# Layer 0 in emission order: attention pairs advance hop by hop between later products, another order of the weight stream, and the last addition moved

## The chip, the core and the metric

The kernel runs on one core of a Trainium2 chip. Its engines run side by side, each with its own queue of instructions in a fixed order, joined by semaphores: TensorE (PE: matmul and transposition; PEld: loading of its weights), VectorE (DVE), ScalarE (ACT), GpSimd (POOL) and SyncE (SP), which issues most transfers. The metric is the device time of one execution in microseconds (us). The profile is taken from one execution.

## What is computed

A decoder trunk of two layers over 256 tokens, width 1024, all in float32, cut here to what matters:

```python
def even_layer(x, mem_n, ...):                       # layer 0
    h = rms_norm(x, norm_g)
    (nq, nkc, nvc, nks, nvs, nkw, nvw, ng, nz, mq, mk, mv, mz, eq, ez) = _split(h @ w_in, EVEN_SPLITS)
    kc = nsa_compress(rot(nkc), pe_k, w1_k, w2_k)
    vc = nsa_compress(heads(nvc), pe_v, w1_v, w2_v)
    gates = jax.nn.sigmoid(ng + gate_b)...
    a_out = nsa_attention(rot(nq), kc, vc, rot(nks), heads(nvs), rot(nkw), heads(nvw), gates)
    b_out = moba_attention(rot(mq), rot(mk), heads(mv))
    m_out = memory_attention(heads(eq), mem_n, w_mem_kv)
    y = jnp.concatenate([a_out * silu(nz), b_out * silu(mz), m_out * silu(ez)], axis=-1) @ w_out
    return x + y

def odd_layer(x, mem_n, ...):                        # layer 1
    h = rms_norm(x, norm_g)
    rq, rk, rv, rz, eq, ez = _split(h @ w_in, ODD_SPLITS)
    ...                                              # retention, 4 heads, and the memory attention again
    return x + y

def reference(...):
    mem_n = rms_norm(mem, mem_norm_g)
    x = even_layer(x, mem_n, ...)
    x = odd_layer(x, mem_n, ...)
    return rms_norm(x, final_norm_g)
```

With 256 tokens the selected blocks and the window of the sparse attention cover all earlier tokens, and the block attention has one block, its own. So each reduces to causal attention: two branches (selected, window) for four pairs of sparse heads, one for four pairs of block heads. The compressed branch has 15 blocks. The memory attention has four heads (two pairs) over 256 memory tokens.

## The kernel before

**Products.** A product multiplies the activations by a 1024x512 piece of weights, which come in four transfers ("units") of 128x1024. Each operand is a sum of a high and a low part in TensorE's fast float type (fp32r), and each product is three matmuls, high times high, high times low, low times high (`mm3`, L138 to L142). The activations are split once. Each unit of weights is split on the chip by `split`: a cast on ScalarE (`whi`, L127) and a subtraction on VectorE (`wlo`, L128). `project` gives tokens on the partitions (two banks of 512 columns, one for each half of the tokens), `project_turned` gives features on the partitions.

**Layer 0.** The first product (`nz`, the sparse group's gate) is written out by hand with the first transfers; its two `pj` banks are read by `gate_path` (L332), once the row scales are known (`rsqrt`, L112; spread over the partitions by L192, copied by L194). Then come `sparse_keys`, `sparse_queries`, `compress` (280 columns: keys and values to compress and the gates; eight additions at L555 put them in the form that two rows of small matmuls take, side by side in the two halves of the array), `memory_queries`, `compressed_scores`, `block_gates`, `block_keys`, `memory_rows`, sparse pairs 0 to 2, the memory keys and attention, `block_queries`, `block_values`, sparse pair 3, four block pairs, and the output product.

**An attention pair** (`causal_pair`, L428; `mem_attention`, L467) handles two heads. TensorE computes the scores of two halves of the tokens (L402, L403); VectorE adds the mask and takes the maxima (L435); ScalarE takes exponentials with their sums (L437); VectorE and ScalarE scale by the inverse sum and the gate (L441 to L448); TensorE transposes (`transposes`, L199); ScalarE copies to `pt` (L449, L492); TensorE multiplies with the values, the two heads side by side in two column halves (`side_by_side`, L105, tile 128x64); `gated` multiplies by the gate and splits the result. A score has the high part of the query in 64 of the 128 rows and its low part in the other 64 (`stack_q`, L341), against the keys stacked likewise (`stack_k`, L348): ScalarE, VectorE and GpSimd prepare these, and each score is two fp32r matmuls.

**What sets the order.** Outside the first transfers a scheduler orders the instructions on every engine from the program's dependencies. Buffers are rings by name: 12 of `v4` (128x1024), three of `whi` and `wlo`, six raw ones, and eight PSUM banks:

```python
BANKS = {"pj": 3, "tr": 1, "s": 2, "t": 1, "o": 1}
```

**The end.** The last product is finished bank by bank (L741 to L747): the two halves of token half 0, the first half of token half 1, and the second half of it in a part of 256 columns and a last one of 256, in a bank of its own. For each, VectorE adds the residual (L879; L876 for the last), ScalarE sums squares (L881); then the root, its inverse (L889), the scaling (L890, L891) and the transfers out (L892, L893).

Of the kernel before, what the change touches and what calls it, by code (L numbers as in the profile page):

```python
# [16 lines left out]
P = 128  # L17
# [4 lines left out]
NV = 12  # L22
NRAW = 6
CUT = 256
BANKS = {"pj": 3, "tr": 1, "s": 2, "t": 1, "o": 1}
# [28 lines left out]
def trunk(  # L54
# [68 lines left out]
    def split(raw, cols, tag=None):  # L123

        hi = tl(tag or "whi", [P, 1024], NV if tag else 3, F32R)[:, :cols]
        lo = tl(tag or "wlo", [P, 1024], NV if tag else 3, F32R)[:, :cols]
        S.copy(hi, raw)  # L127
        V.tensor_tensor(lo, raw, hi.bitcast(F32), ALU.subtract)  # L128
        return hi, lo

    def units(src, idx, cols):

        for u in range(4):
            raw = ahead.pop(0) if ahead else load(tl("raw", [P, 1024], NRAW)[:, : 2 * cols], src[idx + u // 2][:, (u % 2) * 2 * cols : (u % 2 + 1) * 2 * cols])
            wh, wl = split(raw, 2 * cols)
            yield 2 * u, wh, wl

    def mm3(ps, lh, ll, rh, rl, start, stop, shared=False):  # L138

        PE.matmul(ps, lh, rh, start=start, stop=False, skip_group_check=shared)  # L140
        PE.matmul(ps, lh, rl, start=False, stop=False, skip_group_check=shared)  # L141
        PE.matmul(ps, ll, rh, start=False, stop=stop, skip_group_check=shared)  # L142

    def project(src, idx, lhs, cols=512, tag="pj"):

        hi, lo = lhs
        ps = [bank(tag) for _ in range(2)]
        for k0, wh, wl in units(src, idx, cols):
            for tok in range(2):
                for j in range(2):  # L150
# [3 lines left out]
                    mm3(ps[tok][:, :cols], hi[:, kt, ts], lo[:, kt, ts], wh[:, cs], wl[:, cs], kt == 0, kt == KT - 1)  # L154
        return [p[:, :cols] for p in ps]
# [10 lines left out]
    def project_turned(src, idx, lhs):  # L166

        ps = [bank("pj") for _ in range(2)]
        for kt, wh, wl in units(src, idx, 512):
            turned_unit(ps, lhs, wh, wl, (kt, kt + 1), range(4))  # L170
        return ps

    def project_mem(src, idx, lhs):
# [3 lines left out]
        for k0, wh, wl in units(src, idx, 512):  # L177
            turned_unit(ps, lhs, wh, wl, (k0, k0 + 1), range(2))
            for tok in range(2):
# [6 lines left out]
        return ps  # L186

# [28 lines left out]
    def gain_split(raw, g, hi, lo, k0, kts):  # L216
        for kt in kts:
            r = raw[:, kt - k0]
            S.activation(hi[:, kt], r, AF.Copy, scale=g[:, kt : kt + 1])  # L219
            V.scalar_tensor_tensor(lo[:, kt], r, g[:, kt : kt + 1], hi[:, kt].bitcast(F32),  # L220
                                   op0=ALU.mult, op1=ALU.subtract)
# [20 lines left out]
    for tag, shape, bufs, dt in (  # L242
        ("whi", [P, 1024], 3, F32R), ("wlo", [P, 1024], 3, F32R), ("y", [P, 2, 4, T], 2, F32R), ("pt", [P, 2, 512], 2, F32),
        ("ym", [P, 2, 2, T], 1, F32R), ("s2", [P, 2, T], 6, F32), ("rot_a", [P, 512], 2, F32), ("rot_b", [P, 512], 1, F32),
# [24 lines left out]
    for q in range(4):  # L269
        gain_split(xraw[q // 2], vect[:, V_G0 : V_G0 + 8], xh, xl, 4 * (q // 2), range(2 * q, 2 * q + 2))  # L270
# [8 lines left out]
    def row_scale(rows, rstd, width):  # L279
        ss = tl("ss", [P, 2], 2)  # L280
        for tok in range(2):
            S.activation(rows[tok], rows[tok], AF.Square, accum_out=ss[:, tok : tok + 1])
        V.tensor_scalar(ss, ss, 1.0 / width, EPS, op0=ALU.mult, op1=ALU.add)
        rsqrt(rstd, ss, 2)

# [4 lines left out]


    row_scale(xrow, rstd0, D)
# [36 lines left out]
    def gate_path(ps, rb, szT):  # L329

        z = tl("tmp2", [P, 512], 3).rearrange("p (k t) -> p k t", k=2)
        V.scalar_tensor_tensor(z, ps.rearrange("p (k t) -> p k t", k=2), 0.5,  # L332
                               rb.unsqueeze(1).to_broadcast([P, 2, T]), op0=ALU.mult, op1=ALU.mult)
        S.activation(szT, z, AF.Tanh)
        V.scalar_tensor_tensor(szT, szT, 1.0, z, op0=ALU.add, op1=ALU.mult)
# [5 lines left out]
    def stack_q(dst, src):  # L341

        for i in range(2):
            own, other = slice(64 * i, 64 * i + 64), slice(64 - 64 * i, 128 - 64 * i)
            S.copy(dst[own, :, i], src[own])
            V.tensor_tensor(dst[other, :, i], src[own], dst[own, :, i].bitcast(F32), ALU.subtract)

    def stack_k(dst, lo, src):  # L348

        for i in range(2):  # L350
            own, other = slice(64 * i, 64 * i + 64), slice(64 - 64 * i, 128 - 64 * i)
            S.copy(dst[own, :, i], src[own])
            V.tensor_copy(dst[other, :, i], dst[own, :, i].bitcast(F32))
            V.tensor_tensor(lo[own, :, i], src[own], dst[own, :, i].bitcast(F32), ALU.subtract)  # L354
            G.tensor_copy(lo[other, :, i], lo[own, :, i].bitcast(F32))  # L355

    def mem_query(ps, rb, dst):
        e = tl("tmp2", [P, 512], 3).rearrange("p (k t) -> p k t", k=2)
        scaled(ps, rb, 0.125, e)
        stack_q(dst, e)  # L360

    szn = tl("v4", [P, 4, T], NV)
    for i in range(2):
        gate_path(ps_n[i], rb0, szn[:, 2 * i : 2 * i + 2])


    def rot_transpose(ps, name, done):

        for tok in range(2):
            r = rotate(ps[tok], tabs[name][0][:, tok], tabs[name][1][:, tok], 8, 32)  # L370
            b = transposes([r[:, i * P : (i + 1) * P] for i in range(4)], "tr")
            done(b.rearrange("p (k t) -> p k t", t=P), slice(tok * P, (tok + 1) * P))

    def heads_q(ps, plain=None):

        dst = [tl("v4", [P, 2, 2, T], NV, F32R) for _ in range(2)]

        def done(b, ts):
            for i in range(2):
                stack_q(dst[i][:, :, :, ts], b[:, 2 * i : 2 * i + 2])  # L380
            if plain is not None:
                S.copy(plain[:, :, ts], b)

        rot_transpose(ps, "q", done)
        return dst

    def heads_k(ps):
        dst = [tl("v4", [P, 2, 2, T], NV, F32R) for _ in range(2)]
        lo = [tl("v4", [P, 2, 2, T], NV, F32R) for _ in range(2)]

        def done(b, ts):
            for i in range(2):
                stack_k(dst[i][:, :, :, ts], lo[i][:, :, :, ts], b[:, 2 * i : 2 * i + 2])

        rot_transpose(ps, "k", done)
        return dst, lo

    SPAN = (slice(0, P), slice(P, 3 * P))

    def scores(s, q, k, kl):  # L400

        PE.matmul(s, q, k, start=True, stop=False)  # L402
        PE.matmul(s, q, kl, start=False, stop=True)  # L403

    def pair_scores(q, k, kl):

        out = []
        for hh in range(2):
            s = bank("s")
            for tok, a in enumerate(SPAN):  # L410
                scores(s[:, a], q[:, hh, tok * P : (tok + 1) * P], k[:, hh, : a.stop - a.start], kl[:, hh, : a.stop - a.start])
            out.append([s[:, a] for a in SPAN])
        return out

    def branch_scores(q, k, kl):


        s0 = bank("s").rearrange("p (h b n) -> p h b n", h=2, b=2)
        got = [[[None, None], [None, None]] for _ in range(2)]
        for hh in range(2):  # L420
            scores(s0[:, hh], q[:, hh, 0:P], k[:, hh, :, 0:P], kl[:, hh, :, 0:P])
            s1 = bank("s").rearrange("p (b n) -> p b n", b=2)
            scores(s1, q[:, hh, P:T], k[:, hh], kl[:, hh])
            for br in range(2):
                got[br][hh] = [s0[:, hh, br], s1[:, br]]
        return got

    def causal_pair(ss, v, gate, o, first, last):  # L428

        p = tl("p", [P, 2, 512], 2)  # L430
        mx = tl("mx", [P, 2, 2], 3)
        sm = tl("sm", [P, 2, 2], 3)
        for hh in range(2):
            for tok, a in enumerate(SPAN):
                V.tensor_tensor_reduce(p[:, hh, a], ss[hh][tok], cpak[:, C_CAUSAL + a.start : C_CAUSAL + a.stop], -1.0,  # L435
                                       3e38, ALU.add, ALU.min, mx[:, hh, tok : tok + 1])
                S.activation(p[:, hh, a], p[:, hh, a], AF.Exp, bias=mx[:, hh, tok : tok + 1], scale=-1.0,  # L437
                             accum_out=sm[:, hh, tok : tok + 1])
        pt = tl("pt", [P, 2, 512], 2)
        for hh in range(2):  # L440
            V.reciprocal(sm[:, hh], sm[:, hh])  # L441
            if gate is not None:
                V.tensor_tensor(sm[:, hh], sm[:, hh], gate[:, :, hh], ALU.mult)
            for tok, a in enumerate(SPAN):
                if 2 * hh + tok == (0 if gate is None else 3):
                    S.activation(p[:, hh, a], p[:, hh, a], AF.Copy, scale=sm[:, hh, tok : tok + 1])
                else:
                    V.tensor_scalar(p[:, hh, a], p[:, hh, a], sm[:, hh, tok : tok + 1], None, op0=ALU.mult)  # L448
            got = S.copy(pt[:, hh, :384], transposes([p[:, hh, i * P : (i + 1) * P] for i in range(3)]))  # L449
# [546 lines left out]
```

## Time and profile before

| | before |
|---|---|
| median of 3 runs | 443.53 us (442.05 to 443.83) |
| profiled execution | 443.57 us |
| its span (first to last instruction) | 441.8 us |
| transfers | 74.24 MB, mean 168 GB/s |
| TensorE matmul records | 2578 |
| VectorE instructions | 760 |
| ScalarE instructions | 474 |

In the lines of the profile each row names an engine, a line of the kernel, the operation, what it writes and reads (buffers by name, without their numbers), and how often. In a timeline the first number is the start, the second the length in us; a bracket gives the idle time of the engine before it and what ended that. A matmul's record is longer than the distance to the next, since matmuls overlap in the array. A 512-column fp32r matmul comes every 0.23 us, so half a unit of a product, six of them, takes about 1.4 us.

### The profile page before, as it was taken

To read this page: it belongs to the slowest core of one execution; us is meant where nothing else is said; L and a number is where in the kernel's file an instruction comes from. 1 tells how busy PE (TensorE), PEld (TensorE's weight loads), DVE (VectorE), ACT (ScalarE), POOL (GpSimd) and SP (SyncE) were. 2 spreads that over 40 slices of the span, in tenths; PEclk is the share of its full clock that TensorE was granted. 3 is DMA by queue.
4 is the path that set the end of the run, shared out by engine and by line. 5 is a ranking of instruction groups with operands and counts; after the bars stand their busy time and mean duration, and the time that the engine had idled before them with its cause. 6 is when DMAs were issued, how large, how long until landed. Compare 5 with 4: busy or idle time off the path is not lost.

```text
span 441.8 us, 7082 instructions
## 1 busy us (share of the span) xinstructions
PE 423.8 (96%) x2578; PEld 365.6 (83%) x2578; DVE 332.3 (75%) x760; ACT 258.1 (58%) x474; POOL 11.6 (3%) x23
## 2 busy tenths in 40 slices
PE   8999999999997789899999999999999999999994
PEld 7988899898784568667999988888998888888883
DVE  4898989898997685757888875687788487765725
ACT  5756557867667875855646543663633455453714
POOL 0000100002120000000010000000000000000000
PEclk9999999999999799999999999999999999999998
DMA  7965665854525026223555445455545546565402
GB/s 280 397 239 184 226 214 181 294 192 144 185 63 182 0 85 214 86 95 110 178 160 193 145 142 172 161 180 168 187 159 174 171 144 208 168 214 191 144 0 95
DMA packets 22226, 74.24 MB, mean 168 GB/s; under 512 B 2736, under 2 KB 3504, under 8 KB 22192
## 3 DMA queue, kind: packets, MB, share of 16 engines
q1 hardware_dynamic: 21616, 72.95, 49.6%
q10 hardware_dynamic: 576, 0.84, 0.6%
q8 instruction: 20, 0.33, 0.3%
q14 instruction: 14, 0.11, 0.1%
HBM read 72.73 MB, written 1.05 MB: 167 GB/s over the span
## 4 chain that ended last, share of the span: by engine, by line
PE 89%; DVE 4%; ACT 4%; DMA 1%; issue 1%; ACTq 0%
PE pj L140 23%; PE pj L141 23%; PE pj L142 22%; PE t L199 4%; PE o L105 3%; PE s L141 1%; PE s L140 1%; PE s L142 1%; PE tr L140 1%; PE tr L141 1%; PE s L402 1%; PE s L403 1%; PE tr L142 1%; DMA vec<-in_vec 1%; ACT p L437 1%
## 5 line engine op out<-in xcount | busy, mean ns | idle before, releaser
L128 DVE TENSOR_TENSOR wlo<-raw,whi 128x1024 fp32r<-128x1024 f32 (+2 forms) x124 | 145.5, 1177 | 50.4 <-ACT whi L127 49.2
L127 ACT CAST whi<-raw 128x1024 fp32r<-128x1024 f32 (+2 forms) x124 | 124.6, 1007 | 86.3 <-PE pj L142 24.2
L141 PE MATMUL pj<-wlo,big 128*128 128x512 f32 (+2 forms) x264 | 99.0, 375 | 0.1
L142 PE MATMUL pj<-whi,big 128*128 128x512 f32 (+2 forms) x264 | 98.1, 372 | 0.0
L140 PE MATMUL pj<-whi,big 128*128 128x512 f32 (+2 forms) x264 | 92.7, 377 | 0.0
L140 PE MATMUL pj<-big,whi 128*128 128x256 f32 x288 | 80.9, 285 | 0.4 <-ACT big L219 0.3
L141 PE MATMUL pj<-big,whi 128*128 128x256 f32 x288 | 81.2, 285 | 0.0
L142 PE MATMUL pj<-big,wlo 128*128 128x256 f32 x288 | 80.3, 285 | 0.4 <-DVE wlo L128 0.4
L142 PEld LDWEIGHTS pj<-whi,big 128*128 128x128 f32 x264 | 49.7, 188 | 8.4
L141 PEld LDWEIGHTS pj<-wlo,big 128*128 128x128 f32 x264 | 49.7, 188 | 8.3 <-DVE wlo L128 0.3
L140 PEld LDWEIGHTS pj<-big,whi 128*128 128x128 f32 x288 | 54.8, 191 | 1.3 <-ACT big L219 0.7
L140 PEld LDWEIGHTS pj<-whi,big 128*128 128x128 f32 x264 | 49.1, 188 | 8.2 <-issue 0.4
L141 PEld LDWEIGHTS pj<-big,whi 128*128 128x128 f32 x288 | 55.1, 191 | 0.5 <-DVE big L220 0.2
L142 PEld LDWEIGHTS pj<-big,wlo 128*128 128x128 f32 x288 | 54.4, 191 | 0.9 <-DVE wlo L128 0.9
L437 ACT ACTIVATE p<-p,mx 128x256 f32<-128x256 f32 (+1 forms) x48 | 21.4, 449 | 7.0 <-DVE mx L435 6.8
L199 PE MATMUL t<-cst,p 128*128 128x128 f32 x104 | 18.6, 291 | 2.9 <-ACT pt L449 1.5
L199 PEld LDWEIGHTS t<-cst,p 128*128 128x128 f32 x104 | 12.2, 145 | 8.2 <-issue 4.6
L435 DVE CUSTOM_DVE_ANT_0 p<-s,cst 128x256 f32<-128x256 f32 (+1 forms) x48 | 14.7, 352 | 3.6 <-PE t L199 3.3
L449 ACT COPY pt<-t 128x384 f32<-128x384 f32 x24 | 11.4, 477 | 9.7 <-PE t L199 9.4
L105 PE MATMUL o<-pt,s 128*64 128x256 f32 (+1 forms) x96 | 12.4, 385 | 3.8 <-ACT pt L492 1.9
L402 PE MATMUL s<-v,v 128*128 128x256 f32 (+2 forms) x48 | 15.1, 333 | 0.9 <-DVE mx L435 0.7
L355 POOL CAST v<-v 64x256 fp32r<-64x256 f32 (+1 forms) x14 | 9.8, 697 | 193.5 <-DVE v L354 193.5
(287 smaller groups left out, 636.3 us busy)
## 6 DMA issues: line engine op xcount, KB each, us to landing
raw<-in_w SPq DMA_DIRECT2D x91, 512.0 KB, 3.7
raw<-in_wout SPq DMA_DIRECT2D x28, 512.0 KB, 4.1
v<-in_xtok SPq DMA_DIRECT2D x4, 512.0 KB, 6.6
raw<-in_w SPq DMA_DIRECT2D x4, 280.0 KB, 3.3
v<-in_w SPq DMA_DIRECT2D x2, 512.0 KB, 6.5
raw<-in_memT SPq DMA_DIRECT2D x2, 512.0 KB, 4.6
raw<-in_memtok SPq DMA_DIRECT2D x2, 512.0 KB, 5.4
v<-in_grow SPq DMA_DIRECT2D x2, 512.0 KB, 5.7
```

The source lines that it names most:

```text
L105: ins = PE.matmul(out, lhs, rhs, start=start, stop=stop)
L127: S.copy(hi, raw)
L128: V.tensor_tensor(lo, raw, hi.bitcast(F32), ALU.subtract)
L140: PE.matmul(ps, lh, rh, start=start, stop=False, skip_group_check=shared)
L141: PE.matmul(ps, lh, rl, start=False, stop=False, skip_group_check=shared)
L142: PE.matmul(ps, ll, rh, start=False, stop=stop, skip_group_check=shared)
L199: PE.transpose(b[:, i * P : (i + 1) * P], a, ident)
L355: G.tensor_copy(lo[other, :, i], lo[own, :, i].bitcast(F32))
L402: PE.matmul(s, q, k, start=True, stop=False)
L435: V.tensor_tensor_reduce(p[:, hh, a], ss[hh][tok], cpak[:, C_CAUSAL + a.start : C_CAUSAL + a.stop], -1.0, 3e38, ALU.add, ALU.min, mx[:, hh ...
L437: S.activation(p[:, hh, a], p[:, hh, a], AF.Exp, bias=mx[:, hh, tok : tok + 1], scale=-1.0, accum_out=sm[:, hh, tok : tok + 1])
L449: got = S.copy(pt[:, hh, :384], transposes([p[:, hh, i * P : (i + 1) * P] for i in range(3)]))
```

## The change

In the order of the program:

1. The weights come as one stream in a fixed order (`stream`, `coming`). `unit` hands out the next unit and keeps two ahead; `fetch` issues the transfer and ScalarE's cast, `finish` issues VectorE's subtraction later. Of `whi` and `wlo` there are four each.
2. Products and attention are generators. A product yields after every half unit (six matmuls of 512 columns, or twelve of 256), and `turn` then advances every active task by one hop and may start a waiting one; in most of layer 0 it does so every third half unit (`EVERY`). Hops are: scores; masks and maxima; exponentials; scaling; transposes; copies; values; then `gated` in three.
3. From `sparse_keys` to the first output product, TensorE, VectorE and ScalarE keep the order in which the program emits their instructions. Transfers and GpSimd stay with the scheduler, as does all of layer 1.
4. The order of the products is now sparse keys, compression, sparse queries, block keys, block queries, block values, block gates, memory queries, memory keys, and the output product with the sparse rows first and the memory rows last.
5. Scores are one plain fp32 matmul over the 64 rows of a head, two heads side by side in the two row halves (`pair_scores`, tile 64x128). The stacked parts, `stack_q` and `stack_k`, are gone; one copy on ScalarE takes their place (L469). The two branches of a sparse pair are two tasks, and the compressed values are added last (L734).
6. After layer 0 the transition goes by column halves, with the squares behind. The end (`residual`, `gather`, `root_of`, `store`) has its order on VectorE and ScalarE written out; 384 columns of the result are scaled by ScalarE and 640 by VectorE.

```diff
-NV = 12
+NV = 9
+NB = 4
+EVERY = 3
+AHEAD = 2
+NS = 8
...
+    def fetch():
+        src, cols = coming.popleft()
+        raw = ahead.pop(0) if ahead else load(tl("raw", [P, 1024], NRAW)[:, :cols], src)
...
+        S.copy(hi, raw)
+        halves.append((lo, raw, hi))
+        ready.append((hi, lo))
+    def finish():
+        while halves:
+            lo, raw, hi = halves.popleft()
+            V.tensor_tensor(lo, raw, hi.bitcast(F32), ALU.subtract)
+    def unit():
+        while coming and len(ready) <= AHEAD + (len(coming) <= 2):
+            fetch()
+        if len(ready) <= len(halves):
+            finish()
+        return ready.popleft()
+    def turn(start):
+        slot[0] += 1
+        for task in list(active):
+            if next(task, True):
+                active.remove(task)
+        if start and waiting and waiting[0][0] <= made:
+            active.append(waiting.popleft()[1])
+            next(active[-1])
...
-    def scores(s, q, k, kl):
-        PE.matmul(s, q, k, start=True, stop=False)
-        PE.matmul(s, q, kl, start=False, stop=True)
...
+    def pair_scores(q, k, spans):
+        s = [bank("s") for _ in range(2)]
+        todo = []
+        for tok, a in enumerate(spans):
+            for hh in range(2):
+                rows = slice(64 * hh, 64 * hh + 64)
+                todo.append((s[hh][:, a], q[rows, tok * P : (tok + 1) * P], k[rows, : a.stop - a.start], True, True))
+        side_by_side(todo, *readers)
+        readers.clear()
+        return s
...
+    with tc.manual_schedule(engines=MANUAL):
+        drive(sparse_keys())
+        drive(compress())
+        drive(sparse_queries())
+        waiting.append(({"qT", "kcBD", "gates"}, making(compressed_scores(), "pcT")))
+        waiting.extend(({"qT", "kT", "gates"} | ({"pcT"} if br == 2 else set()), sparse_branch(pr, br))
+                       for pr in range(4) for br in (1, 2))
+        drive(block_keys(), EVERY)
+        drive(block_queries(), EVERY)
...
-    acc = out_project(0, [(ym, 2), (yn, 4), (yb, 4)])
+        acc = yield from out_project([(yn, 4, 1, None), (yb, 4, 3, lambda: started(0)), (ym, 2, 0, drain)])
...
+        residual(1, 0, 0, 512, acc[1][0])
+        store(0, r)
+        residual(1, 1, 512, 512 - CUT, acc[1][1])
+        gather(1, 2)
+        residual(1, 2, 1024 - CUT, CUT, acc[2][:, 512 - CUT :])
+        store(1, root_of(1, 2))
```

Three places show what that moves. In the rows a number behind a name tells one buffer from another. The first place is VectorE's queue just behind the sparse keys, before (`s_335`, `s_336`: the two banks of the sparse keys; `pj_72`, `pj_73`: those of the first product; `wlo_550`: a unit of the compression).

```order
L213 TENSOR_TENSOR rot_a_86<-rot_a_86,rot_b_87 128x256
L128 TENSOR_TENSOR wlo_472<-raw_469,whi_471 128x1024
L194 COPY rb_90<-tr_287 128x256
L212 TENSOR_TENSOR rot_b_415<-s_336,stk_319 128x256
L332 SCALAR_TENSOR_TENSOR tmp_65_327<-pj_72,rb_90 128x512
L332 SCALAR_TENSOR_TENSOR tmp_66_331<-pj_73,rb_90 128x512
L213 TENSOR_TENSOR rot_a_414<-rot_a_414,rot_b_415 128x256
```

The same place of the change (`s_346` is the second bank of the keys, `wlo_432` and `wlo_460` are units of the compression, `pj_427` is the compression's first bank):

```order
L302 TENSOR_TENSOR rot_a_438<-s_346,ctk_318 128x256
L303 TENSOR_TENSOR rot_b_439<-s_346,stk_319 128x256
L304 TENSOR_TENSOR rot_a_438<-rot_a_438,rot_b_439 128x256
L156 TENSOR_TENSOR wlo_432<-raw_429,whi_431 128x560
L285 COPY rb_90<-tr_287 128x256
L156 TENSOR_TENSOR wlo_460<-raw_457,whi_459 128x560
L442 SCALAR_TENSOR_TENSOR tmp_65_327<-pj_72,rb_90 128x512
L442 SCALAR_TENSOR_TENSOR tmp_66_329<-pj_73,rb_90 128x512
```

L442 reads the banks of the first product behind all six rotations of the keys, and TensorE's second bank of the compression needs one of these banks after the first six matmuls of that product; before, the last rotation stood behind it and TensorE had three units of the queries' first half to do.

The second place is TensorE's queue in the attention pairs, before, at the end of the memory group (`t`: transposes, `s`: scores, `o`: values):

```order
L199 MATMUL t_1402<-cst_65,p_1377 128x128 x3
L105 MATMUL o_1330<-pt_1388,s_23_85 64x256 x2
L105 MATMUL o_1330<-pt_1388,s_23_85 64x128 x2
L199 MATMUL t_1602<-cst_65,p_1579 128x128 x4
L402 MATMUL s_1863<-v_79_405,v_100_506 128x256
L403 MATMUL s_1863<-v_80_406,v_100_506 128x256
```

And in the change, a part of the block queries' product (`pj_982`, `pj_983`):

```order
L111 MATMUL o_938<-pt_963,s_85_419 64x256 x2
L111 MATMUL o_938<-pt_963,s_85_419 64x128 x2
L734 MATMUL o_938<-s_174_842,vcr_94 128x256
L290 MATMUL t_1053<-cst_65,p_968 128x128 x3
L290 MATMUL tr_1057<-cst_65,p_968 128x128 x3
L211 MATMUL pj_982<-whi_930,big_70 128x512
L212 MATMUL pj_982<-wlo_931,big_70 128x512
L213 MATMUL pj_982<-whi_930,big_71 128x512
L211 MATMUL pj_982<-whi_930,big_70 128x512
L212 MATMUL pj_982<-wlo_931,big_70 128x512
L213 MATMUL pj_982<-whi_930,big_71 128x512
L111 MATMUL s_1090<-s_23_85,v_133_670 128x128
```

Between the hops of the pairs stand six matmuls of a product each time.

The third place is VectorE's end, before (`pj_4259`, `tr_4260` and `s_4537`: the three banks of token half 1):

```order
L891 TENSOR_SCALAR p_4602<-p_4602,ss_849_4601 128x512
L879 TENSOR_TENSOR v_398_2137<-pj_4259,v_398_2137 128x512
L883 TENSOR_TENSOR p_4619<-v_398_2137,v_788_4255 128x512
L879 TENSOR_TENSOR v_398_2137<-tr_4260,v_398_2137 128x512
L884 TENSOR_SCALAR ss_853_4618<-ss_853_4618 128x1
L876 TENSOR_TENSOR v_398_2137<-s_4537,v_398_2137 128x256
```

and in the change (`pj_4120`, `tr_4121` and `s_4386` are these banks):

```order
L1058 TENSOR_TENSOR v_375_1920<-pj_4120,v_375_1920 128x512
L1061 TENSOR_TENSOR p_4451<-v_375_1920,v_784_4116 128x512
L1078 TENSOR_SCALAR p_4450<-p_4450,ss_841_4452 128x640
L1058 TENSOR_TENSOR v_375_1920<-tr_4121,v_375_1920 128x512
L1061 TENSOR_TENSOR p_4451<-v_375_1920,v_784_4116 128x256
L1065 TENSOR_SCALAR ss_842_4453<-ss_842_4453 128x1
L1067 SCALAR_TENSOR_TENSOR ss_842_4453<-ss_842_4453 128x1
L1058 TENSOR_TENSOR v_375_1920<-s_4386,v_375_1920 128x256
```

The scaling of token half 0 now stands behind the first addition of half 1, and a gain multiplication and two sums stand ahead of the last addition.

More of the change, by code (lines that the diff above doesn't have):

```diff
@@ L129, in split, with is_free, take, give @@
         return hi, lo
[L131 to L136, printed above, removed]
+    coming, ready, halves = deque(), deque(), deque()
+    def fetch():
+        src, cols = coming.popleft()
+        raw = ahead.pop(0) if ahead else load(tl("raw", [P, 1024], NRAW)[:, :cols], src)
+        if len(coming) < 2:
+            hi, lo = [tl("v4", [P, 1024], NV, F32R) for _ in range(2)]
+        else:
+            hi = tl("whi", [P, 1024], NB, F32R)[:, :cols]
+            lo = tl("wlo", [P, 1024], NB, F32R)[:, :cols]
+        S.copy(hi, raw)
[11 more added lines that the diff above has]
+        return ready.popleft()
+    waiting, active, made, slot, free = deque(), [], set(), [0], {}
+    def turn(start):
[6 more added lines that the diff above has]
+            next(active[-1])
+    def is_free(tag):
+        return free.get(tag, 0) <= slot[0]
+    def take(*tags):
+        while not any(is_free(tag) for tag in tags):
+            yield
+        tag = [tag for tag in tags if is_free(tag)][0]
+        free[tag] = 1 << 30
+        return tag
+    def give(tag, after=1):
+        free[tag] = slot[0] + after
+    def making(task, *names):
+        yield from task
+        made.update(names)
+    def drive(stage, every=1):
+        for i, _ in enumerate(stage):
+            turn(i % every == 0)
+    def drain(n=0):
+        while len(waiting) + len(active) > n:
+            turn(True)
     def mm3(ps, lh, ll, rh, rl, start, stop, shared=False):
@@ L186, in project_mem, with now @@
         return ps
+    def now(stage):
+        while True:
+            slot[0] += 1
+            try:
+                next(stage)
+            except StopIteration as end:
+                return end.value
     def spread(col, dst):
@@ L428, in causal_pair @@
-    def causal_pair(ss, v, gate, o, first, last):
+            yield
+            yield
+            tag = yield from take("tr", "t")
+            b = transposes([r[:, i * P : (i + 1) * P] for i in range(4)], tag)
+            yield
+            S.copy(dst[:, :, tok * P : (tok + 1) * P], b.rearrange("p (k t) -> p k t", t=P))
+            give(tag)
+    SPAN = (slice(0, P), slice(P, 3 * P))
+    readers = []
+    def pair_scores(q, k, spans):
[8 more added lines that the diff above has]
+        return s
@@ new lines, in turn_probabilities, with leave @@
+    def turn_probabilities(p, cols, blocks):
+        pt = tl("pt", [P, 2, 512], 2)
+        tags = ("t",) if crowded else ("t", "tr")
+        held = []
+        def leave():
+            for hh, tag, b in held:
+                got = S.copy(pt[:, hh, :cols], b)
+                give(tag)
+            held.clear()
+            return got
+        for hh in range(2):
+            if hh and not any(is_free(tag) for tag in tags):
+                yield
+                leave()
+            tag = yield from take(*tags)
+            held.append((hh, tag, transposes([p[:, hh, i * P : (i + 1) * P] for i in blocks], tag)))
+        yield
+        got = leave()
+        yield
+        return pt, got
@@ L430, in causal_pair @@
+    crowded = False
+    def causal_pair(q, k, v, gate, out, first, last, close=None):
+        ss = pair_scores(q, k, SPAN)
+        yield
         p = tl("p", [P, 2, 512], 2)
@@ L437, in causal_pair @@
+        yield
+        for hh in range(2):
+            for tok, a in enumerate(SPAN):
                 S.activation(p[:, hh, a], p[:, hh, a], AF.Exp, bias=mx[:, hh, tok : tok + 1], scale=-1.0,
                              accum_out=sm[:, hh, tok : tok + 1])
[L439 to L449, printed above, removed]
+        yield
@@ L450, in causal_pair @@
+        softmax_scale(p, sm, SPAN, gate, 0 if gate is None else 3)
+        yield
+        pt, got = yield from turn_probabilities(p, 384, range(3))
+        o = out()
         side_by_side([(o[hh * 64 : hh * 64 + 64, kt * P : T], v(hh, kt), pt[:, hh, kt * T : kt * P + T],
                        first and kt == 0, last and kt == 1) for kt in range(2) for hh in range(2)], got)
+        if close is not None:
+            yield from close(o)
     def gated(o, szT, y, kt):
+        yield
         yf = tl("yf", [P, T], 2)
@@ L618, in memory_queries @@
-    def memory_queries():
-        nonlocal eqS, szm
-        eqS = tl("v4", [P, 2, 2, T], NV, F32R)
-        szm = tl("s2", [P, 2, T], 6)
-        ps_e = project_turned(w512, W["e0"], (xh, xl))
-        mem_query(ps_e[0], rb0, eqS)
-        gate_path(ps_e[1], rb0, szm)
+        yield
+        pcT = tl("s2", [P, 2, T], NS)
+        tag = yield from take("tr", "t")
+        b = transposes([pc[:, tok, 4 * u : 4 * u + 4].rearrange("p h n -> p (h n)") for u in range(2) for tok in range(2)], tag)
+        yield
@@ L650, in memory_group, with post @@
-    def memory_group():
-        nonlocal eqS, szm, memkS, memkL, memv, ym
-        ym = tl("ym", [P, 2, 2, T], 1, F32R)
-        mem_attention(eqS, memkS, memkL, memv, szm, ym)
+        tag = yield from take("tr", "t")
+        b = bank(tag)
+        for tok in range(2):
+            PE.matmul(b[:, tok * P : (tok + 1) * P], rstdm[:, tok : tok + 1].to_broadcast([P, P]), ident, start=True, stop=True)
+        yield
+        V.tensor_copy(rbm, b[:, :T])
+        give(tag)
+    def memory_keys():
+        nonlocal memk, memv
+        assert {"mh", "rbm"} <= made
+        ps = yield from project_mem((mh, ml))
+        memk = tl("s2", [P, 2, T], NS)
+        memv = tl("s2", [P, 2, T], NS)
+        def post():
+            mem_keys(ps, rstdm, rbm, memk, memv)
+            yield
+        active.append(making(post(), "memk"))
```

567 lines of the change are left out of this document (306 added, 261 removed).

## The prediction

> **What bounds the kernel now.** First the page: the share of each engine, TensorE's forty slices, the chain of waits.
>
> ```profile
> span 441.8 us, 7082 instructions
> PE 423.8 (96%) x2578; PEld 365.6 (83%) x2578; DVE 332.3 (75%) x760; ACT 258.1 (58%) x474; POOL 11.6 (3%) x23
> PE   8999999999997789899999999999999999999994
> PE 89%; DVE 4%; ACT 4%; DMA 1%; issue 1%; ACTq 0%
> ```
>
> TensorE is busy for 96% of the span and carries 89% of the chain. So time can come only from TensorE's own work, from its idle time or from its clock. The slices are full but for the ends and one place, a third to a half of the way in; behind it, in layer 1, there is no gap. The windows give that place in microseconds (columns: length, busy us of PE, PEld, DVE, ACT, POOL with counts, granted clock, DMA share, GB/s):
>
> ```profile
> 132.00:143.00 11.00, 7.83 (x51) 5.19 (x51) 9.15 (x37) 8.20 (x26) 0.00 (x0) 0.97 0.58 188
> 143.00:154.00 11.00, 8.49 (x48) 6.12 (x50) 6.77 (x23) 9.22 (x31) 0.00 (x0) 0.72 0.00 0
> 154.00:165.00 11.00, 9.89 (x61) 7.26 (x57) 8.36 (x31) 8.78 (x26) 0.00 (x0) 1.00 0.22 63
> ...
> 176.00:187.00 11.00, 9.86 (x69) 7.77 (x68) 8.05 (x32) 9.00 (x27) 0.00 (x0) 1.00 0.31 97
> 187.00:198.00 11.00, 10.43 (x60) 7.67 (x59) 5.94 (x20) 7.09 (x18) 0.00 (x0) 1.00 0.29 95
> 198.00:209.00 11.00, 9.94 (x65) 8.15 (x65) 7.96 (x13) 5.52 (x12) 0.00 (x0) 1.00 0.29 97
> ```
>
> From 132 to 209 us TensorE is idle for 3.17 + 2.51 + 1.11 + 1.14 + 0.57 + 1.06 = 9.6 us (none in the row left out). The clock of 0.72 in one window costs 0.28 x 11 = 3.1 us more. DVE and ACT have room in every row (at most 9.2 of 11 us), so the gaps are latency. TensorE's timeline shows whose:
>
> ```profile
> 133.81 0.87 PE L105 MATMUL o<-pt,s 128*64 128x256 f32 x8
> 134.62 0.55 PE L199 MATMUL t<-cst,p 128*128 128x128 f32 x3
> ...
> 137.65 0.55 PE L199 MATMUL t<-cst,p 128*128 128x128 f32 x3
> 137.95 0.48 PE L402 MATMUL s<-v,v 128*128 128x512 f32 x1
> 138.27 0.40 PE L403 MATMUL s<-v,v 128*128 128x512 f32 x1
> 138.50 0.28 PE L402 MATMUL s<-v,v 128*128 128x256 f32 x1
> 138.62 0.28 PE L403 MATMUL s<-v,v 128*128 128x256 f32 x1
> ...
> 141.74 0.61 PE L199 MATMUL t<-cst,p 128*128 128x128 f32 x3 [1.35 <-DVE p L448]
> 142.92 1.55 PE L105 MATMUL o<-pt,s 128*64 128x256 f32 x8 [0.57 <-ACT pt L449]
> ...
> 145.31 0.41 PE L403 MATMUL s<-v,v 128*128 128x256 f32 x1
> 145.53 0.41 PE L402 MATMUL s<-v,v 128*128 128x256 f32 x1
> ```
>
> These are the steps of an attention pair, one behind the other with no product between. A block of transposes with nothing to wait for afterwards occupies 0.30 us (137.65 to 137.95), but its record is 0.55 long; so each gap is some 0.25 longer than its bracket. There are 11 such gaps from 132 to 209: 2.7 us.
>
> **The change: what it can win.** The pairs now advance a hop per half unit of product, so the products stand in these gaps. All of it together is 9.6 + 3.1 + 2.7 = **15.4 us**. Bounds: 9.6, if the clock and the hidden part stay, and 15.4. I take 15.4, since 68 half units stand beside the pairs. The removed splitting of queries and keys (ACT, DVE, POOL) lies beside TensorE's work and is worth nothing by itself.
>
> **Scores.** Records of 512 columns follow each other in 0.23 us (138.27 to 138.50), of 256 in 0.12 (138.50 to 138.62), two per score. A causal pair is now 0.69, a memory pair 0.93: 12 x 0.69 + 4 x 0.93 = 12.0 us. The new ones are plain fp32, as in these four records of two 128x256 matmuls (layer 1's retention; the second row is the group, with its mean in ns):
>
> ```profile
> 264.54 1.02 PE L811 MATMUL s<-v,v 128*128 128x256 f32 x4
> L811 PE MATMUL s<-v,v 128*128 128x256 f32 x16 | 4.1, 378 | 0.0
> ```
>
> Less the last record's own 378 ns, three intervals take 0.64: 0.215 a record, two records and 0.43 a matmul. If the two row halves run together, a causal pair (128 + 256 columns) takes 0.645 and a memory pair 0.86: 11.2 us in all; one after the other 22.4. No row of before shows row halves; the nearest is L105, column halves: eight records that would take 1.29 in a row, and 0.645 side by side, take 0.81 (133.81 to 134.62). I take side by side, and 0.16 a block for entering and leaving: 11.2 + 16 x 0.16 - 12.0 = **+1.8 us** (bounds -0.8 and +13).
>
> The Trainium skill, page "TensorEngine Tiling (Array Packing)", section "Tiling Modes", says that tiles run in parallel and that changing the tiling mode drains the engine. L105's 0.81 against 0.645 agrees with both; were the drain free, the sum would end 2.6 us lower.
>
> **The first products.** The compression product now directly follows the sparse keys. The `pj` banks are three, two held by the first product until `gate_path` (before L332, now L442) has read them. The scheduler had put all of the first token half of the queries into the third; in emission order the compression's second half comes after six matmuls. On VectorE L442 stands behind tables, six rotations, two splits and a copy:
>
> ```profile
> 27.07 0.23 DVE L324 TENSOR_SCALAR ctk<-trig,rstd 128x32 f32<-128x32 f32 x1
> ...
> 28.82 1.22 DVE L128 TENSOR_TENSOR wlo<-raw,whi 128x1024 fp32r<-128x1024 f32 x1
> 29.95 0.41 DVE L211 TENSOR_TENSOR rot_a<-s,ctk 128x256 f32<-128x256 f32 x1
> 30.29 0.41 DVE L212 TENSOR_TENSOR rot_b<-s,stk 128x256 f32<-128x256 f32 x1
> ...
> 33.08 1.27 DVE L332 SCALAR_TENSOR_TENSOR tmp<-pj,rb 128x512 f32<-128x512 f32 x2
> 39.41 0.74 DVE L128 TENSOR_TENSOR wlo<-raw,whi 128x560 fp32r<-128x560 f32 x1 [0.42 <-ACT whi L127]
> 29.34 0.39 PE L142 MATMUL s<-whi,big 128*128 128x512 f32 x1
> 30.93 0.61 PE L192 MATMUL tr<-cst,rstd 128*128 128x128 f32 x4
> ```
>
> From 27.0, tables 1.75 (27.07 to 28.82), six rotations at 0.34, two splits of 560 at 0.65, a copy 0.34, the first gate 0.64: 33.1. TensorE ends the keys at 29.6 and needs six matmuls of 280 columns (280/512 of 0.227, 0.12 each) and 0.4 for the row scales: ready at 30.7. Stall **2.5 us** (bounds 0, if the rotations start early, and 4). Its cover before was the query half, now emitted later.
>
> Further on, the side-by-side block of the compression waits for eight additions (L555, now L663) behind two splits (1.13 each, 28.82 to 29.95); 18 matmuls at 0.227 = 4.1 us cover them:
>
> ```profile
> L555 DVE TENSOR_TENSOR tmp<-o,vec 64x240 f32<-64x240 f32 x8 | 3.2, 406 | 0.1
> L213 DVE TENSOR_TENSOR rot_a<-rot_a,rot_b 128x512 f32<-128x512 f32 (+2 forms) x10 | 5.9, 592 | 0.0
> ```
>
> 3.2 + 2 x 1.13 - 4.1 = **1.4 us** (bounds 0 and 3). The second bank of each projection waits for the rotation of the last one's first bank: three operations of about 0.6, 1.8 against the 1.36 of six matmuls. 0 to 0.4 each, six times; I take 0.15: **0.9 us**.
>
> **Hops of a pair.** Emission order also fixes ACT and DVE, so a step queues behind whatever was emitted before it.
>
> ```profile
> 133.20 0.49 ACT L437 ACTIVATE p<-p,mx 128x256 f32<-128x256 f32 x1
> ...
> 133.69 0.39 ACT L437 ACTIVATE p<-p,mx 128x128 f32<-128x128 f32 x1
> ...
> 134.08 1.03 ACT L127 CAST whi<-raw 128x1024 fp32r<-128x1024 f32 x1
> 135.20 0.48 ACT L449 COPY pt<-t 128x384 f32<-128x384 f32 x1
> ```
>
> Four exponentials are 2 x 0.49 + 2 x 0.39 = 1.8 us, a cast 0.95, two copies some 0.75 (0.48 each, less the tenth by which records here run into the next): 3.5 where all three meet, against two slots of 1.36. The L105 block behind them then waits up to 0.7 us, and the next product behind it in TensorE's queue. Nothing to 0.7 for 16 pairs; I take 0.2: **3.2 us**.
>
> **The end.**
>
> ```profile
> 435.09 0.69 DVE L879 TENSOR_TENSOR v<-tr,v 128x512 f32<-128x512 f32 x1
> 435.88 0.42 DVE L876 TENSOR_TENSOR v<-s,v 128x256 f32<-128x256 f32 x1
> 437.47 0.49 DVE L891 TENSOR_SCALAR p<-p,ss 128x512 f32<-128x512 f32 x1
> ```
>
> The first token half's scaling (L891, 0.49 for 512 columns, so 0.6 for 640) now stands ahead of the second of these additions, and the last addition behind a sum that waits for ACT's square. 0.6 + 0.3: **+0.9 us** (bounds 0 and 1.3).
>
> Layer 1 has no gap to close: nothing. **Sum:** -15.4 + 1.8 + 2.5 + 1.4 + 0.9 + 3.2 + 0.9 = -4.7. The profiled execution is 443.57 us (span 441.8 and 1.8 around it), the median 443.53: **438.9 us**.
>
> **Rivals.** (A) *The hops hide everything.* DVE and ACT have idle time in every window, and the softmax of a pair spreads over some nine half units, 12 us, where the four exponentials take 1.8. Then the four stalls (2.5, 1.4, 0.9, 3.2 = 8.0) are gone: 430.9 us. Against it: in-order queues.
>
> (B) *In-order queues give the gain back.* At the bound of 0.7 us for each of 16 pairs the hops cost 11.2, 8.0 more: 446.9 us, slower. ACT is at 9.2 of 11 us in the window 143:154, which speaks for it; the pairs' spacing of three slots speaks against.
>
> (C) *Row halves run one after the other.* +11.2: 450.1 us, slower. It decides from 6.8 of these 11.2 us on (445.7), so from 60% not overlapped. L105 speaks against, though for columns.
>
> (D) *The clock falls again, elsewhere.* After brackets of 1.35 and 0.57 close together the rows at 145 us come 0.215 apart instead of 0.12: half rate, though no gap before them reached 2 us. A stall of 2.5 early on could do it; once or twice 3.1: 442.0 to 445.1, no change.
>
> The Trainium skill, page "TensorE: Matmul & The Clock Gate", Part 1, lets the clock halve after an idle window of about 3.4 us. The trace has it after shorter gaps; by the rule read as one unbroken gap, D would not occur and the forecast stand.
>
> That the change does not fill the gaps is excluded by the order, where products stand between the hops.
>
> **How the numbers follow.** Forecast, 435 to 443: 0.46. A 0.22, D 0.12, B 0.12, C 0.08. A measurement of this kernel tells apart about 0.5%, 2.2 us: faster is below 441.3. Of the forecast 0.40 lies there, with A 0.62. Same: 0.06 of the forecast, D, and 0.04 of B, 0.22. Slower: 0.16. The range reaches from A's 430.9, less 2 for a drain that costs nothing, to B's 447; C is left out.
>
> **What would show it.** Windows of the first 220 us without idle time but for 30 to 34 and near the compression; a clock of 1.00 throughout; the blocks of four score matmuls at 0.65 to 0.8 us (C: 1.3); brackets before the second line of each `o` block, from ACT `pt`, up to 0.7; last addition near 437. The forecast is wrong if brackets in the pair stage sum to over 8 us, or to nearly nothing.

## The result, and the profile after

| | before | after |
|---|---|---|
| median | 443.62 us (442.05 to 443.83, 4 runs) | 436.61 us (435.71 to 437.19, 4 runs) |
| profiled execution | 443.57 us | 436.11 us |
| its span | 441.8 us | 434.3 us |
| last matmul starts | 435.25 us | 427.78 us |

After to before is 0.9848 (95% interval 0.9817 to 0.9878): 6.7 us faster (7.0 between the medians), more than the 4.7 that were forecast, inside the range of 429 to 447.

The page after: busy shares, TensorE's slices, the clock.

```profile
span 434.3 us, 7010 instructions
PE 423.2 (97%) x2610; PEld 360.9 (83%) x2610; DVE 306.8 (71%) x689; ACT 241.7 (56%) x445; POOL 1.9 (0%) x9
PE   8988999999999999999999999999999999999994
PEclk9999999999999999999999999999999999999999
```

The hole a third of the way in is closed, and a small one stands in the third and fourth slices. The windows of the changed kernel (the columns as in the prediction's windows) put numbers to it:

```profile
22.00:44.00 22.00, 19.36 (x111) 16.80 (x110) 19.76 (x54) 15.06 (x23) 0.53 (x1) 1.00 0.77 266
44.00:66.00 22.00, 21.52 (x163) 17.88 (x163) 15.51 (x27) 8.71 (x15) 0.00 (x0) 1.00 0.54 178
132.00:143.00 11.00, 11.00 (x94) 9.61 (x92) 7.35 (x26) 6.66 (x21) 0.00 (x0) 1.00 0.47 154
143.00:154.00 11.00, 11.00 (x94) 9.64 (x93) 9.14 (x31) 7.03 (x21) 0.00 (x0) 1.00 0.34 103
198.00:209.00 11.00, 11.00 (x96) 11.00 (x95) 9.53 (x21) 6.24 (x11) 0.00 (x0) 1.00 0.58 193
```

From 66 us to the end of layer 0 TensorE shows no idle time. What is left is 2.64 us in the window from 22 and 0.48 in the next. TensorE's and VectorE's timelines show both places, and one piece of the pair stage:

```profile
32.94 1.28 DVE L442 SCALAR_TENSOR_TENSOR tmp<-pj,rb 128x512 f32<-128x512 f32 x2
30.76 0.38 PE L213 MATMUL pj<-whi,big 128*128 128x280 f32 x1
33.77 0.37 PE L211 MATMUL pj<-whi,big 128*128 128x280 f32 x1 [2.63 <-DVE tmp L442]
47.66 2.06 PE L111 MATMUL o<-tmp,v 128*64 128x30 f32 x64 [0.47 <-issue]
...
85.71 0.40 PE L213 MATMUL pj<-whi,big 128*128 128x512 f32 x1
85.95 0.49 PE L290 MATMUL tr<-cst,p 128*128 128x128 f32 x3
86.37 0.93 PE L111 MATMUL s<-s,v 64*128 64x128 f32 x8
87.22 0.50 PE L211 MATMUL pj<-whi,big 128*128 128x512 f32 x1
87.56 0.39 PE L212 MATMUL pj<-wlo,big 128*128 128x512 f32 x1
```

The bracket of 2.63, ended by L442, is the stall that the prediction put at 2.5. The prediction's own terms give 33.1 - 30.7 = 2.4. In the pair stage no row has a bracket. A block of scores of a causal pair takes 0.85 us (86.37 to 87.22): the two row halves run together, since by the prediction's rate they would take 1.29 one after the other. The product behind it needs 0.34 for its first matmul (87.22 to 87.56) in place of 0.23.

Summing, for each matmul record, the distance to the start of the next one shows where TensorE's time went, waits included (us; the sum is the difference of the last matmuls' starts):

| kind | before | after | difference |
|---|---|---|---|
| transposes | 26.2 | 18.4 | -7.8 |
| scores | 17.4 | 15.1 | -2.3 |
| values of pairs | 15.9 | 13.7 | -2.2 |
| product of 280 columns | 6.7 | 9.2 | +2.6 |
| other products | 350.7 | 352.6 | +1.9 |
| the rest | 17.2 | 17.4 | +0.2 |
| all | 433.9 | 426.5 | -7.5 |

At the end, VectorE's timeline and TensorE's last matmul, after:

```profile
425.22 0.69 DVE L1058 TENSOR_TENSOR v<-pj,v 128x512 f32<-128x512 f32 x1 [0.65 <-PE pj L213]
426.56 0.55 DVE L1078 TENSOR_SCALAR p<-p,ss 128x640 f32<-128x640 f32 x1
427.02 0.68 DVE L1058 TENSOR_TENSOR v<-tr,v 128x512 f32<-128x512 f32 x1
428.41 0.42 DVE L1058 TENSOR_TENSOR v<-s,v 128x256 f32<-128x256 f32 x1
427.78 0.28 PE L213 MATMUL s<-v,y 128*128 128x256 f32 x1
```

The last addition starts 0.63 us behind the start of the last matmul; before it was 435.88 - 435.25 = 0.63 as well.

### The profile page after: what moved, and what is told of

Read it like the earlier page. It is cut to its first block, busy times and chain, and to the rows that moved or that the text cites. A ratio compares the mean times of both kernels' runs of the same rounds, so it can differ in the third digit from the quotient of the medians.

```text
span 434.3 us, 7010 instructions
## 1 busy us (share of the span) xinstructions
PE 423.2 (97%) x2610; PEld 360.9 (83%) x2610; DVE 306.8 (71%) x689; ACT 241.7 (56%) x445; POOL 1.9 (0%) x9
## 4 chain that ended last, share of the span: by engine, by line
PE 90%; DMA 4%; DVE 3%; ACT 1%; issue 1%; DVEq 0%
PE pj L211 24%; PE pj L213 23%; PE pj L212 23%; PE o L111 4%; PE s L111 3%; PE t L290 3%; DMA raw<-in_xT 2%; DMA v<-in_xtok 2%; PE tr L290 2%; PE tr L211 1%; PE tr L213 1%; PE tr L212 1%; PE s L997 1%; PE o L734 1%; DVE wlo L156 1%
## 5 line engine op out<-in xcount | busy, mean ns | idle before, releaser
L156 DVE TENSOR_TENSOR wlo<-raw,whi 128x1024 fp32r<-128x1024 f32 (+1 forms) x118 | 141.9, 1206 | 52.6 <-ACT whi L148 50.8
L148 ACT CAST whi<-raw 128x1024 fp32r<-128x1024 f32 (+1 forms) x118 | 121.8, 1035 | 91.2 <-PE pj L213 42.6
L211 PE MATMUL pj<-whi,big 128*128 128x512 f32 (+2 forms) x264 | 100.0, 381 | 2.6 <-DVE tmp L442 2.6
L213 PE MATMUL pj<-whi,big 128*128 128x512 f32 (+2 forms) x264 | 98.2, 372 | 0.0
L211 PE MATMUL pj<-big,whi 128*128 128x256 f32 x288 | 83.3, 291 | 0.4 <-ACT big L309 0.4
L212 PE MATMUL pj<-big,whi 128*128 128x256 f32 x288 | 81.2, 283 | 0.0
L541 ACT ACTIVATE p<-p,mx 128x128 f32<-128x128 f32 (+1 forms) x48 | 21.3, 448 | 4.2 <-DVE mx L535 4.2
L508 ACT COPY pt<-t 128x384 f32<-128x384 f32 (+1 forms) x19 | 9.7, 508 | 17.0 <-PE t L290 16.9
L535 DVE CUSTOM_DVE_ANT_0 p<-s,cst 128x128 f32<-128x128 f32 (+1 forms) x48 | 14.2, 353 | 5.4 <-PE s L111 3.7
L211 PE MATMUL pj<-whi,y 128*128 128x512 f32 x42 | 17.0, 409 | 0.0
L213 PE MATMUL pj<-whi,y 128*128 128x512 f32 x42 | 16.4, 391 | 0.0
L212 PE MATMUL pj<-wlo,y 128*128 128x512 f32 x42 | 16.3, 391 | 0.0
L497 DVE TENSOR_SCALAR p<-p,sm 128x256 f32<-128x256 f32 (+1 forms) x48 | 12.7, 322 | 0.5
```

The costliest lines, as they stand in the source:

```text
L213: return PE.matmul(ps, ll, rh, start=False, stop=stop, skip_group_check=shared)
L508: got = S.copy(pt[:, hh, :cols], b)
L535: got = V.tensor_tensor_reduce(p[:, hh, a], ss[hh][:, a], cpak[:, C_CAUSAL + a.start : C_CAUSAL + a.stop], -1.0, 3e38, ALU.add, ALU.min, m ...
```

## The experiments

The theory at the outset was that of the prediction: products between the hops are the gain, the stacking that is gone is worth nothing by itself, and the stall at the compression is only a matter of order.

**Scores and stacking alone.** The kernel before, its order left to the scheduler, with the new scores and without stacking:

```diff
-                stack_q(dst[i][:, :, :, ts], b[:, 2 * i : 2 * i + 2])
+            S.copy(dst[:, :, ts], b)
...
-        PE.matmul(s, q, k, start=True, stop=False)
-        PE.matmul(s, q, kl, start=False, stop=True)
+                todo.append((s[hh][:, a], q[rows, tok * P : (tok + 1) * P], k[rows, : a.stop - a.start], True, True))
+        side_by_side(todo, *readers)
```

> The kernel before with the new scores alone: queries and keys are not stacked, each score is one plain matmul over 64 rows with the two heads in the two row halves; the order stays with the scheduler. Theory (products in the hops are the gain): the gaps of the pair stage stay, the waits for the stacking go; 441 to 444.5. Rival (scores and stacking are the gain): 437 to 439, with idle time from 130 to 210 us below 4 us.

Measured: 438.59 us, 0.9896 of before (0.9862 to 0.993). The rival's time, not the theory's: 4.6 us of the gain come without any product being moved by hand. The theory's gaps did not stay: from 132 to 209 us TensorE is idle for 4.4 us in place of 9.6, a little above the rival's 4.

**The stacking back, for nothing.** In that kernel the stacked parts ("dead stacks" below) are computed all the same, into buffers that no score reads.

```diff
             S.copy(dst[:, :, ts], b)
+            for i in range(2):
+                stack_q(dead()[:, :, :, ts], b[:, 2 * i : 2 * i + 2])
```

> The kernel before with plain scores, as in the run of that name, but the stacked parts of queries and keys are computed all the same by ScalarE, VectorE and GpSimd into buffers that nothing reads (with 10 buffers of v4 in place of 12, to make room). Theory A (the stacking cost by its load on the three engines' queues): the gain is gone, 441.5 to 444. Theory B (it cost by lying between the rotation and the scores, or the scores themselves are cheaper in the gaps): 438 to 440.

Measured: 446.09 us. Its last matmul starts at 434.65 of a span of 444.6, so 9.95 us remain behind it against 6.5 elsewhere: here the end itself is late. Whether the 10 buffers of `v4` do that was not taken apart, so this run says little; its time lies above both theories. It was repeated with the stacks in layer 0 alone, into a spare buffer, and with all 12.

> As the run with dead stacks, but with all 12 buffers of v4: in layer 0 the stacked parts are computed into one spare buffer that nothing reads, the scores are the plain ones. The run with 10 buffers had 3.4 us more after the last matmul, which has nothing to do with stacking. Theory A (the stacking cost by its load on the queues of ScalarE, VectorE and GpSimd): the last matmul is 2 us or more later than with plain scores alone, 441 to 444. Theory B (it cost only by lying between the rotation and the scores, or through the scores themselves): within 1 us of 438.6.

Measured: 444.82 us, 1.0043 of before (1.0026 to 1.0059), 6.2 us above the plain scores and 0.8 above theory A's range. In the profiles the last matmul starts 4.3 us later (435.98 against 431.69). The windows of the two, plain scores first, then with dead stacks:

```profile
132.00:154.00 22.00, 19.18 (x107) 13.25 (x109) 13.45 (x37) 15.35 (x43) 0.00 (x0) 0.85 0.52 172
154.00:176.00 22.00, 22.00 (x127) 15.99 (x123) 13.18 (x49) 14.53 (x40) 0.00 (x0) 1.00 0.22 73
```

```profile
132.00:154.00 22.00, 17.16 (x106) 11.77 (x105) 18.71 (x50) 19.19 (x51) 1.22 (x2) 1.00 0.48 168
154.00:176.00 22.00, 19.83 (x116) 14.26 (x117) 12.26 (x50) 12.84 (x38) 0.00 (x0) 1.00 0.15 49
```

No score reads the stacks, so they can't delay one as its input, and theory B is out. They load ScalarE (15.35 to 19.19 us of 22) and VectorE (13.45 to 18.71), and TensorE's idle time from 132 to 176 goes from 2.8 to 7.0 us. Theory A has the direction, but the load alone is not shown to be the cause, since the traces show two other things that came with the stacks. The first is a bank: TensorE waits for VectorE's stacking subtraction (L346 there), which still reads the bank that the next transposes write (before, one such wait of 0.98). With dead stacks:

```profile
143.77 0.66 PE L199 MATMUL tr<-cst,rot_a 128*128 128x128 f32 x4 [1.19 <-DVE y L346]
```

The second is TensorE's own order, which the scheduler made anew for each program. These windows count the product matmuls that write `pj` (their time and number stand behind the length; then clock, DMA share and GB/s). They reach from the third addition of compressed values (`o<-s,vcr`) to the output product: before, plain scores, dead stacks:

```profile
139.05:156.60 17.55, 0.00 (x0) 0.81 0.03 12
133.22:154.90 21.68, 7.27 (x28) 0.84 0.52 170
141.66:157.45 15.79, 0.47 (x1) 1.00 0.51 183
```

With plain scores 28 product matmuls stand between the last steps of these pairs, 6.4 us at 0.23 each; with dead stacks one does, and before none. So a part of what the plain scores gained can itself be products between the hops, put there by the scheduler. How much is the load, the bank and the order was not taken apart. The plain scores by themselves, with the stacks still computed, bring nothing: 1.9 us more than before, to which the copies that they add may belong.

**Products taken out of the hops.** The changed kernel, with sparse and block pairs only after the last projection:

```diff
-        waiting.extend(({"qT", "kT", "gates"} | ...), sparse_branch(pr, br)) ...)
         drive(block_keys(), EVERY)
         ...
         drive(memory_keys(), EVERY)
+        waiting.extend(...)
+        n = 0
+        while len(waiting) + len(active) > 0:
+            turn(n % EVERY == 0)
+            n += 1
```

> The changed kernel, but the compressed scores, the sparse pairs and the block pairs start only after the last projection, three hops apart as before, with no product between them; everything else (plain scores, no stacking, pinned order) stays. Theory (the gain is that products fill the hops): 12 pairs with some 4 us of hops each against 2.5 us of their own TensorE work leave 10 to 20 us idle, and the clock may fall again: 446 to 460. Rival (the gain comes from the plain scores and the stacking that is gone): within 3 us of 436.6.

Measured: 462.8 us. Its windows where the pairs stand alone:

```profile
132.00:154.00 22.00, 16.76 (x104) 10.24 (x105) 11.03 (x62) 15.66 (x55) 0.00 (x0) 0.77 0.01 1
154.00:176.00 22.00, 15.02 (x118) 9.07 (x117) 13.36 (x75) 16.74 (x60) 0.00 (x0) 1.00 0.00 1
```

This is a single execution. TensorE is idle for 12.2 us in these two windows, and the clock is at 0.77 in one. Without products the hops cost some 26 us, beyond what was expected; so in this program the products do hide about that much. It does not say that the scheduler's order before lost as much.

**The order given back to the scheduler.** The changed program without the pinned order, here and at the first output product:

```diff
-    with tc.manual_schedule(engines=MANUAL):
+    if True:
```

> The changed kernel with the pinned order of layer 0 given back to the scheduler, which sees the same program. Theory (products between the hops are the gain, and pinning costs the 2.63 us at the compression): the bracket at 33 us goes, a few gaps return; 434 to 440. Rival (pinning is the gain): gaps as before the change, 441 to 446.

Measured: 439.98 us, 0.9924 of before (0.9903 to 0.9945). Just inside the theory's range, but 3.4 us above the changed kernel although the stall at the compression is gone: transposes take 21.2 us and scores 17.8 by the sums above, against 18.4 and 15.1. The intervals of the two ratios lie apart, so pinning is a part of the gain.

**The stall at the compression.** The row scales are spread, and the first product's banks read, while the keys are still multiplied:

```diff
-    spread(rstd0, rb0)
...
-    now(gate_path(ps_n, rb0, szn))
...
+    def first_gate():
+        for _ in range(5):
+            yield
+        spread(rstd0, rb0)
+        yield
+        yield from gate_path(ps_n, rb0, szn)
...
     with tc.manual_schedule(engines=MANUAL):
+        active.append(first_gate())
         drive(sparse_keys())
```

> The changed kernel with one thing moved: the row scales are spread and the first product's gate banks are read while the sparse keys are still being multiplied, ahead of their rotations. Theory (the 2.63 us bracket before the compression's second bank is only the place of L442 in VectorE's queue): the bracket goes, no other of over 0.5 us comes, and the time falls by 2 to 2.6 us, to about 434.2. Rival (the rotations and the compression's own steps are then late by the same amount): the idle time shows up before 60 us at another place and the time stays at 436.6 within 0.7.

Measured: 435.43 us, 0.982 of before (0.9793 to 0.9848), between the theory's time and the rival's. The bracket of 2.63 went, but TensorE's timeline had three in its place:

```profile
26.99 0.71 PE L283 MATMUL tr<-cst,rstd 128*128 128x128 f32 x4 [0.87 <-DVE rstd L127]
33.66 0.30 PE L290 MATMUL tr<-cst,rot_a 128*128 128x128 f32 x1 [0.32 <-DVE rot_a L304]
34.69 0.55 PE L290 MATMUL tr<-cst,rot_a 128*128 128x128 f32 x3 [0.73 <-DVE rot_a L304]
```

Most of the wait (1.92 of 2.63) had moved, as the rival said, to instructions placed too early. So these were put later: six half units before the scales, four hops before the keys' transposes.

> As the run with the gate early, with the row scales spread one half unit later and the transposes of the sparse keys two half units later, where the trace of that run had its new brackets (0.87 on VectorE's row scale, 0.32 and 0.73 on the rotation). Theory (these brackets are only places in the order): the idle time before 44 us falls from 2.1 to under 0.7 us and the time to 433.9 to 434.9. Rival (VectorE is late as a whole there, and the wait moves on to the compression): idle time of 2 us somewhere before 66 us, 436 or more.

Measured: 434.66 us, 0.9806 of before (0.9777 to 0.9835). The time is the theory's, but the profiled execution, the slowest of the five (435.53), still has 2.0 us of idle time before 44 us, where under 0.7 was expected; 0.85 of it is waiting for a `wlo`. In the repeat below it is 0.5. Since the time stands close to the interval of the change, both were run once more on one chip.

> The changed kernel once more, on the same chip as the next run: 436.6 within 0.7.

> The kernel with the gate early and the key transposes later once more, beside the changed kernel: 1.5 to 2.3 us below it, if the stall at the compression was worth its bracket; within 0.7, if the difference so far was one of chips.

Measured: the changed kernel 437.33 us (0.987; 0.9847 to 0.9892), this one 434.24 (0.9802; 0.9785 to 0.982), 3.1 us less, more than the 1.5 to 2.3 expected. The window from 22 to 44 us, the changed kernel first:

```profile
22.00:44.00 22.00, 19.58 (x106) 17.50 (x105) 18.39 (x51) 13.79 (x21) 0.00 (x0) 0.92 0.78 265
```

```profile
22.00:44.00 22.00, 21.68 (x123) 18.79 (x121) 21.06 (x55) 14.42 (x23) 0.53 (x1) 1.00 0.83 300
```

2.4 us of idle time became 0.3, and the clock of 0.92 is 1.00. The clock is what exceeds the bracket: the one execution of the control with a mean clock of 0.998 took 436.05, 1.8 us more than this kernel's median. A mean clock of 0.994 or less stands in 7 of the 14 executions that have the stall (the changed kernel's two measurements and the run on its end below), and in none of the 16 of the three runs with the gate early. This is the fastest version of the study.

**The end.** The changed kernel with the end of before:

```diff
-        residual(1, 0, 0, 512, acc[1][0])
-        store(0, r)
-        residual(1, 1, 512, 512 - CUT, acc[1][1])
...
+        for i, (c0, n) in enumerate(cuts):
+            ...
```

> The changed kernel with the end of before (residual additions, sums and scaling left to the scheduler, two halves of 512 columns). My prediction put the new end at +0.9 us; the trace of the change shows 6.5 us from the last matmul to the end of the span, as before. If the new end costs, this is 0.5 to 1 us faster than 436.6; if it gains, 0.3 to 1 us slower; if the two are alike, within 0.3.

Measured: 436.69 us, 0.9849 of before (0.9821 to 0.9877): alike. Behind the last matmul its profile has 6.2 us, the change 6.5.

## Why the prediction came out as it did

The direction and the main term were right. The size was short, because most of the stalls that were set against the gain did not come. The time lies in the forecast's 435 to 443, but the prediction's own sign of being wrong came true as well: the brackets in the pair stage sum to nothing. The nearness of the number is in part luck. Stalls of 5.9 us that did not come (hops 3.2, banks 0.9, end 0.9, compression 0.9) are offset in part by a gain that was 1.3 short and by 1.4 that was not in the sum.

| term | forecast | measured, and by what |
|---|---|---|
| gaps, clock and scores together | -15.4 + 1.8 = -13.6 | -12.3 (transposes, scores, values in the sums) |
| stall before the compression | +2.5 | +2.6 (the bracket of 2.63) |
| side-by-side block of the compression | +1.4 | +0.5 (the bracket of 0.47) |
| banks of the projections | +0.9 | 0 (no bracket) |
| hops of the pairs | +3.2 | 0 (no bracket) |
| other products | not in the sum | +1.4 (+1.9, less the 0.5 above) |
| end | +0.9 | 0 (6.55 and 6.52 us behind the last matmul) |
| the rest | not in the sum | +0.2 |
| sum | -4.7 | -7.5 (as in the sums; the rows are rounded) |

- **What failed: the hops.** "I take 0.2: 3.2 us" supposed that exponentials, a cast and copies often meet on ScalarE. No bracket shows that they delayed TensorE: the copies have a slot of their own between them and the values. (A wait that fits into the overlap of two records shows no bracket; it would be in the first row of the table.) Rival A was right on this, the banks and nearly on the compression; with the early stall kept, 433 would have been its time, and the shorter gain and the other products took 2.7 us of it.
- **The other products** lost on entering and leaving them. If a matmul of 512 columns counts 0.2275 us and one of 256 0.1205, the first matmuls of their stretches cost 6.8 us more than that in 74 places, against 5.2 in 68 before; the last ones 3.2 (the bracket of 0.47 among them) against 1.5; those in between 0.3 against 1.6.
- **What failed where the scheduler has the order: "The removed splitting of queries and keys lies beside TensorE's work and is worth nothing by itself."** With plain scores its removal is worth 6.2 us (444.82 against 438.59). By which way, load, bank or the scheduler's order, is open, as said there. It is open as well what the removal is worth in the change's pinned order, where the stacks were not put back. Pinning and products between the hops brought 2.0 us more by the medians (438.59 to 436.61; the intervals overlap) while paying 2.6 for the early stall; without that stall, 4.4 (434.24, intervals apart).
- **The early stall** was right in place, cause and size, and could be removed.
- **The scores.** Rival C is out: 0.85 us a block, 0.81 forecast. A whole sum of 15.1 us stands against 13.8 forecast (11.2 and 16 times 0.16): entering and leaving take 0.21 a block, not the 0.16 of L105, and one memory block of layer 1 stands in two parts, which costs 0.6.
- **Rival D** came true in part, at less than half of its 3.1 us. The profiled execution keeps its clock, but in that of the control the window from 22 us has 0.92 and TensorE's compression product takes 10.5 us by the sums in place of 9.2. The four executions of the first measurement have mean clocks of 0.998, 0.997, 0.993 and 0.994 and times of 436.11, 435.71, 437.10 and 437.19: the lower clock goes with about 1.2 us.
- **The end**: the forecast laid the scaling on top of the times of before, where VectorE's first addition of token half 1 starts at 433.65, 1.6 us ahead of the last matmul. TensorE's order there is another now: 24 matmuls of 256 columns stand behind that bank, where 16 did, and its addition starts 2.56 us ahead (425.22 against 427.78), which pays for the scaling in between. "Last addition near 437" did not go with the forecast's own sum either: 435.88 - 4.7 is 431.2. It was 428.41.

## What to carry to other kernels

Work on an engine with idle time is not free where a chain of short steps, to which the bound engine waits, passes through that engine: take it away, or run it with its result unread, before calling it hidden. Then compare the bound engine's order in the two programs, because a scheduler that sees other work also places the rest anew. When an order is pinned, look for readers of a scarce bank that stand behind other work in their own queue; here one such place cost its full bracket, and moving it too early opened others. And count what each interruption of a long run of matmuls costs on the way in and out, not only what it fills.

## What was not expected of the hardware

A single gap of 2.4 to 2.6 us at the same place went with a lower granted clock in one profile (0.92 over the window from 22 to 44 us, behind 2.42) and with 1.00 in another (behind 2.63), and the kernel with dead stacks kept 1.00 through gaps of 4.4 us in the 11 us from 143, where the kernel before had 0.72 with 2.5. What decides between them stays open. And the first 512-column matmul of a product behind other work took 0.32 us on the mean of 39 entries, against 0.23 within a product; before the change it was 0.31 in 40.
